# Triangular diagonal blocks of a gated delta rule: 32x32 blocks solved on GpSimd instead of 16x16 blocks with a doubling step on TensorE

## The chip, the cores and the metric

The kernel runs on one core of a Trainium2 chip. The metric is device microseconds of one execution. The kernel before takes 3029.99 us (median of 3 runs, 3028.96 to 3030.83).

## What is computed

One residual layer over 1024 time steps of width 2048: RMSNorm, one combined projection, two branches (an S5 state-space scan and a gated DeltaNet), merge gates, output projection, residual, final RMSNorm. All is float32. The change lies in the DeltaNet branch alone, 8 heads of width 128:

```
a_mat = where(strict, beta * kk * decay, 0)             # per chunk of time steps, strictly lower
sol   = triangular_solve(a_mat, [v*beta, k*beta*exp(gc)], lower, unit_diagonal)
u_c, w_c = sol[..., :dv], sol[..., dv:]
step: v_new = u_i - w_i @ state ; o = qd_i @ state + qk_i @ v_new
      state = state * gl_i + kd_i^T @ v_new
```

The kernel does not solve for the right-hand sides. It builds the inverse of the unit triangular matrix (I + A) for each chunk and multiplies with it. Its chunks have 128 steps.

## The kernel before

**Passes and columns.** The sequence is worked off in two passes of 512 steps. A pass runs through a list of column blocks of 128 projection columns (k, q, v, z and two gate columns for each head, and one u or zs column); each is a row of matmuls on TensorE of 128x512, three for each of 16 slices of the contraction (weights split in a high and a low part: high x high, high x low, low x high). The weights come by SP DMAs of 512 KB into three buffers `raw` (line 397), ScalarE copies the high part `whi` and VectorE subtracts for the low part `wlo`, five buffers each, prepared four chunks (of four slices) ahead (`LA`, line 391).

**What runs between the columns.** All other work stands in lanes (line 444), as Python generators. After each slice of a column, `pump` (line 475) lets every lane issue its next piece, if a planner's clock (class `Clock`, lines 31 to 91, with the costs of lines 140 to 143) says that what the piece before made is ready by TensorE's planned time, 0.2 us of margin added (`step`, line 455). So the order on each engine is fixed when the program is built, by planned times; on the chip, semaphores hold back what comes too early. A DMA is planned at 0.45 us of issue on SP and some 1.1 us of latency after its transfer; a GpSimd two-input operation at 0.14 us and 2.1 ns for each element of its row. Before the columns of head i, `drain` (lines 1529, 1530) issues what is left of the heads up to i-2.

**Lane prep, `d_prep` (line 1090), once for each head and pass, 16 times in all.** Each works on 4 chunks of 128 steps at once, so on 128x512 tiles:
1. GpSimd and TensorE make the decay factors E. Once the head's q column is there, TensorE transposes k (`pK`), ScalarE squares q and k, and TensorE sums the squares by a product with `ones` (`pQ`, line 1116).
2. TensorE multiplies k with k and q (`pA`), VectorE masks and scales: LU, for each chunk c the matrix LU[s, c, t], upper triangular, as the transpose of A.
3. LU goes to DRAM (`lu_d`, line 1139), and the 32 diagonal blocks of 16x16 (8 in each of 4 chunks) come back with one block in each of 32 partitions.
4. GpSimd inverts the blocks by 15 steps of substitution, two operations each (line 1152), and copies a transposed form.
5. Both forms go to DRAM (`tu_d`, two DMAs), and both come back into 128x512 tiles `Tm` and `U` (two DMAs, lines 1173 and 1174). Off the blocks these DRAM areas hold zeros, written once at the start (`zero_tu`).
6. TensorE doubles the blocks from 16 to 32: 16 products of 32x32 (`pG`), two VectorE operations, 32 products of 32x32 (`pU`, line 1188), eight ScalarE copies of 32x128.
7. TensorE doubles from 32 to 64 (8 and 16 products of 32x32) and from 64 to 128 (4 and 4 of 64x64).

**Lane chain, `d_chain` (line 1240),** takes U, which is now the full inverse, through the recurrence over the four chunks. Lane s5 carries the scans of the other branch, mainly on VectorE.

The profile's times for these pieces all have line 135, the recording helper, so they are told apart by tile names: `M` is the block in which all of the head's tiles (LU, E, mi, U, v, kq) lie, `p` a PSUM bank.

Of the kernel before, what the change touches and what calls it, by code (L numbers as in the profile page):

```python
# [93 lines left out]
class Timed:  # L94
# [3 lines left out]
    def __getattr__(self, name):  # L98
# [45 lines left out]
        "memset": _VF, "reciprocal": {"V": (0.07, 8.3e-3)}, "iota": _VG, "matmul": None, "transpose": None, "dma_start": None}  # L144
# [3 lines left out]
def kernel(  # L148
# [90 lines left out]
    off16 = cpool.tile([P, 2, 16], F32, name="off16")  # L239
    id32 = cpool.tile([P, 32], F32, name="id32")  # L240
    G.memset(off16, 0.0)
    for b in range(4):
        s32 = slice(32 * b, 32 * b + 32)
        G.tensor_copy(id32[s32, :], ident[s32, s32])
        G.memset(off16[s32, 0, :], -1.0)
        G.affine_select(off16[s32, 0, :], off16[s32, 0, :], pattern=[[0, 16]], compare_op=ALU.is_ge,
                        fill=0.0, base=-16, channel_multiplier=1)
# [29 lines left out]
    lu_d = [dram.tile([4, 129, P], F32, name=f"lu_d{i}") for i in range(2)]  # L277
    tu_d = [[dram.tile([4, 129, P], F32, name=f"tu_d{i}{j}") for j in range(2)] for i in range(2)]
# [717 lines left out]
    def d_views(mb):  # L996
# [93 lines left out]
    def d_prep(h, ps_):  # L1090
# [48 lines left out]
        SP.dma_start(rows(lud), LU)  # L1139
        yield  # L1140
        mif = mi.rearrange("p c n -> p (c n)")
        Ef = E.rearrange("p c n -> p (c n)")
        ba = mif[0:32, 0:256].rearrange("p (i m) -> p i m", i=16)
        btm = mif[0:32, 256:512].rearrange("p (i m) -> p i m", i=16)
        bx = Ef[0:32, 0:256].rearrange("p (i m) -> p i m", i=16)
        bu = Ef[0:32, 256:512].rearrange("p (i m) -> p i m", i=16)
# [33 lines left out]
        B4 = [slice(32 * b, 32 * b + 32) for b in range(4)]  # L1180
# [502 lines left out]
```

## Time and profile before

| | |
|---|---|
| median of 3 runs | 3029.99 us |
| the profiled execution | 3029.73 us |
| its span | 3027.8 us |
| TensorE busy | 2974.2 us (98%) |
| VectorE, ScalarE, GpSimd busy | 55%, 38%, 15% |
| mean granted clock | 0.993 |

One execution was profiled. Its span runs from the first to the last instruction; 1.9 us of the execution's time lie around it. Busy time of TensorE is the time in which at least one matmul is under way, and since matmuls overlap, a row's own mean is longer than the time that it takes from the engine. What a group of small matmuls takes is therefore read from the starts of the rows on both sides of it.

### The profile page before, as it was taken

How to read it: one execution, taken by the hardware profiler on the slowest of the kernel's cores; microseconds unless marked ns; L12 is line 12 of the kernel's file. 1: busy time of each engine (PE TensorE's matmuls, PEld its weight loads, DVE VectorE, ACT ScalarE, POOL GpSimd, SP SyncE). 2: the span in 40 equal slices, each digit the busy share in tenths (PEclk: the TensorE clock that was granted, in tenths of full speed). 3: DMA queues.
4: the chain of work that ended last, by engine and by line, in shares of the span. 5: the costliest groups of instructions: out<-in, count | busy, mean ns of one | idle time of the engine just before them, and what ended most of it. 6: DMA issues, size and time to landing. Idle time of an engine off the chain costs nothing.

```text
span 3027.8 us, 42544 instructions
## 1 busy us (share of the span) xinstructions
PE 2974.2 (98%) x16030; PEld 2391.6 (79%) x16030; DVE 1662.4 (55%) x3082; ACT 1152.2 (38%) x2483; POOL 449.3 (15%) x857
## 2 busy tenths in 40 slices
PE   8989999999999999999999999999999999999998
PEld 6877777777777888888878777777777788888887
DVE  5746676777777522553454575567557633226542
ACT  5434544554454222334333333333433322223331
POOL 4412222122200000000033221222112000000000
PEclk9999999999999999999999999999999999999999
DMA  6525444444445644446354344444444464445541
GB/s 168 133 57 154 122 121 130 111 117 122 133 135 166 191 122 120 144 134 238 119 160 134 108 114 115 133 114 117 119 126 120 123 207 122 122 122 153 197 151 56
DMA packets 582143, 405.02 MB, mean 134 GB/s; under 512 B 55161, under 2 KB 515122, under 8 KB 580018
## 3 DMA queue, kind: packets, MB, share of 16 engines
q1 hardware_dynamic: 579634, 393.92, 45.3%
q0 software_dynamic: 2304, 8.39, 0.8%
q8 instruction: 126, 2.06, 0.3%
q14 instruction: 79, 0.65, 0.1%
HBM read 335.66 MB, written 66.58 MB: 133 GB/s over the span
## 4 chain that ended last, share of the span: by engine, by line
PE 85%; DVE 7%; POOL 2%; ACT 2%; issue 1%; DMA 1%; SPq 0%; DVEq 0%; POOLq 0%; ACTq 0%
PE p L135 85%; DVE G0a L135 2%; POOL M L135 2%; DVE M L135 2%; DVE wlo L135 1%; DVE tmp L135 1%; ACT M L135 1%; DMA raw<-in_w_in_dram 0%; DVE Y L135 0%; POOL smalls L135 0%; DMA M<-tu_d 0%; SPq L135 0%; ACT whi L135 0%; ACT L135 0%; ACT tmp L135 0%
## 5 line engine op out<-in xcount | busy, mean ns | idle before, releaser
L135 PE MATMUL p<-X,whi 128*128 128x512 f32 (+1 forms) x4432 | 1398.7, 398 | 1.9 <-DVE whi L135 0.8
L135 DVE TENSOR_TENSOR wlo<-raw,whi 128x512 fp32r<-128x512 f32 x920 | 631.0, 698 | 700.9 <-ACT whi L135 700.1
L135 PEld LDWEIGHTS p<-X,whi 128*128 128x128 f32 (+1 forms) x4432 | 802.8, 188 | 177.1 <-issue 19.9
L135 PE MATMUL p<-X,wlo 128*128 128x512 f32 (+1 forms) x2184 | 854.2, 391 | 8.0 <-DVE wlo L135 7.9
L135 ACT ACTIVATE whi<-raw 128x512 fp32r<-128x512 f32 x917 | 557.7, 625 | 512.6 <-PE p L135 485.0
L135 PE MATMUL p<-Y,whi 128*128 128x512 f32 (+1 forms) x1808 | 568.8, 396 | 1.9 <-ACT whi L135 1.1
L135 PEld LDWEIGHTS p<-X,wlo 128*128 128x128 f32 x2184 | 411.7, 189 | 97.6 <-DVE wlo L135 9.1
L135 PEld LDWEIGHTS p<-Y,whi 128*128 128x128 f32 (+1 forms) x1808 | 329.9, 187 | 72.8 <-ACT whi L135 2.6
L135 PE MATMUL p<-Y,wlo 128*128 128x512 f32 x896 | 349.8, 390 | 0.0
L135 POOL TENSOR_SCALAR smalls<-smalls 128x4 f32<-128x4 f32 (+1 forms) x58 | 15.7, 270 | 1603.8 <-DVE smalls L135 1109.4
L135 ACT ACTIVATE tmp<-p 128x512 f32<-128x512 f32 x160 | 95.5, 597 | 401.8 <-PE p L135 391.9
L135 POOL TENSOR_TENSOR M<-M 32x28 f32<-32x28 f32 (+8 forms) x492 | 190.7, 388 | 289.4 <-DMA M<-lu_d 194.2
L135 DVE TENSOR_TENSOR G0a<-G0a 128x256 f32<-128x256 f32 (+1 forms) x432 | 212.3, 528 | 3.4
L135 PEld LDWEIGHTS p<-M 32*32 32x32 f32 (+2 forms) x3072 | 153.5, 123 | 72.6 <-ACT M L135 32.7
L135 PEld LDWEIGHTS p<-Y,wlo 128*128 128x128 f32 x896 | 168.3, 188 | 36.5 <-DVE wlo L135 0.4
L135 PE MATMUL p<-M 32*32 32x32 f32 (+3 forms) x3072 | 187.2, 215 | 7.5 <-ACT M L135 3.8
L135 ACT ACTIVATE M<-p 32x128 f32<-32x128 f32 (+3 forms) x337 | 99.3, 298 | 159.9 <-PE p L135 156.2
L135 DVE SCALAR_TENSOR_TENSOR tmp<-tmp,vec 128x512 f32<-128x512 f32 x144 | 115.6, 803 | 11.9 <-ACT tmp L135 8.5
L135 DVE TENSOR_TENSOR_SCAN G0a<-rho,scar,G0a 128x256 f32<-128x256 f32 x128 | 89.7, 742 | 0.0
L135 DVE TENSOR_TENSOR G0a<-p,G0a 128x512 f32<-128x512 f32 x128 | 82.0, 682 | 13.4 <-PE p L135 10.8
L135 PE MATMUL p<-whi,G0a 128*128 128x512 f32 x280 | 88.5, 391 | 0.0
L135 PE MATMUL p<-whi,X 128*128 128x512 f32 x256 | 82.2, 393 | 0.0
(210 smaller groups left out, 2655.4 us busy)
## 6 DMA issues: line engine op xcount, KB each, us to landing
raw<-in_w_in_dram SPq DMA_DIRECT2D x324, 512.0 KB, 4.0
raw<-in_w_out_dram SPq DMA_DIRECT2D x56, 512.0 KB, 3.9
raw<-in_dn_w_up_dram SPq DMA_DIRECT2D x32, 512.0 KB, 4.1
raw<-in_s_w_up_dram SPq DMA_DIRECT2D x32, 512.0 KB, 3.8
td_d<-tmp SPq DMA_DIRECT2D x32, 256.0 KB, 2.0
M<-tu_d SPq DMA_DIRECT2D x32, 256.0 KB, 3.8
cs_d<-G0a SPq DMA_DIRECT2D x32, 256.0 KB, 2.3
yg_d<-G0a SPq DMA_DIRECT2D x64, 128.0 KB, 2.4
```

The lines of the kernel that those rows point to most:

```text
L135: return f(*a, **k)
```

## The change

The diagonal blocks that GpSimd inverts are 32x32 instead of 16x16, and step 6, the doubling from 16 to 32, is gone.

- LU's 16 diagonal blocks (4 in each chunk) are written by four DMAs, one for each group of 32 partitions, so that each block lies as 4 KB in one piece. Each block is read into eight partitions: 128 partitions with 4 KB each, over E and mi, which now lie side by side.
- Each partition solves four of a block's 32 columns: 31 steps of two operations on 128 partitions, with 4 x 31 elements in a row at first and 4 x 1 in the end. The right-hand side is the identity, which one more DMA reads from DRAM into the first quarter of U; the second quarter holds the products.
- One form of the result is written and read back (one DMA each instead of two). VectorE makes the other by a transpose of 32x32 blocks, 128x512 in one instruction.
- The constants `off16` and `id32` are no longer made, two of four areas are zeroed at the start, and the planner gets a cost for VectorE's transpose.

```diff
-        SP.dma_start(rows(lud), LU)
-        yield
...
-        SP.dma_start(ba, diag_blocks(lud))
-        G.memset(mif[0:32, 256:512], 0.0)
-        G.memset(mif[0:32, 256:512:17], 1.0)
-        yield
-
-        for j in range(15):
-            n = 15 - j
-            a = ba[:, j, j + 1:16].unsqueeze(2).broadcast_to([32, n, j + 1])
-            b = btm[:, j:j + 1, 0:j + 1].broadcast_to([32, n, j + 1])
-            tt(bx[:, 0:n, 0:j + 1], a, b, MUL, eng=G)
-            tt(btm[:, j + 1:16, 0:j + 1], btm[:, j + 1:16, 0:j + 1], bx[:, 0:n, 0:j + 1], SUB, eng=G)
+        for b in range(4):
+            SP.dma_start(part(lud, b * 1024, (32, 32), (4096, 4), (1, 32)),
+                         LU[32 * b:32 * b + 32, :, 32 * b:32 * b + 32])
+        yield
+
+
+        lb = dw["Emi"].rearrange("p (j t) -> p j t", j=32)
+        Uf = U.rearrange("p c n -> p (c n)")
+        iu, ix = (Uf[:, i * P:(i + 1) * P].rearrange("p (m t) -> p m t", m=4) for i in range(2))
+        SP.dma_start(dw["Emi"], part(lud, 0, (1024, 16), (0, 8), (1, 1024)))
+        SP.dma_start(Uf[:, 0:P], part(idg_d, 0, (0, 16), (P, 8), (1, P)))
+        yield
+        for j in range(31):
+            n = 31 - j
+            a = lb[:, j:j + 1, j + 1:32].broadcast_to([P, 4, n])
+            b = iu[:, :, j:j + 1].broadcast_to([P, 4, n])
+            tt(ix[:, :, 0:n], a, b, MUL, eng=G)
+            tt(iu[:, :, j + 1:32], iu[:, :, j + 1:32], ix[:, :, 0:n], SUB, eng=G)
             if j % 3 == 2:
                 yield
-        G.tensor_copy(bu, btm.rearrange("p i m -> p m i"))
-        yield
-        SP.dma_start(diag_blocks(tud[0]), btm)
-        SP.dma_start(diag_blocks(tud[1]), bu)
+        SP.dma_start(part(tud, 0, (4128, 16), (512, 8), (P, 4), (1, 32)), iu)
...
-        SP.dma_start(Tm, rows(tud[0]))
-        SP.dma_start(U, rows(tud[1]))
-        yield
-
-        pG = bank(5)
+        SP.dma_start(U, rows(tud))
+        yield
+        V.transpose(Tm.rearrange("p c n -> p (c n)"), U.rearrange("p c n -> p (c n)"))
         gs = mi
-        g3 = mi[:, :, 0:32]
...
-        for b in B4:
-            for c in range(4):
-                PE.matmul(pG[b, c * 32:(c + 1) * 32], lhsT=LU[b, c, b], rhs=Tm[b, c, b], start=True, stop=True)
...
-        for b in B4:
-            S.activation(U[b, :, b], pU[b, 0:P].rearrange("p (c n) -> p c n", c=4), AF.Copy)
-        for b in B4:
-            S.activation(Tm[b, :, b], pU[b, P:2 * P].rearrange("p (c n) -> p c n", c=4), AF.Copy)
         yield
```

TensorE's queue at the end of the prep of head 4 in the second pass, before: `M_1700_13069` is the head's block, `p_2185_16984` the bank of the column under way.

```order
L135 MATMUL p_2185_16984<-X_1462_11596,wlo_16955 128x512
L135 MATMUL p_2194_17060<-M_1700_13069 32x32 x16
L135 MATMUL p_2185_16984<-X_1462_11596,whi_16985 128x512 x2
L135 MATMUL p_2185_16984<-X_1462_11596,wlo_16986 128x512
L135 MATMUL p_2185_16984<-X_1462_11596,whi_16985 128x512 x2
L135 MATMUL p_2185_16984<-X_1462_11596,wlo_16986 128x512
L135 MATMUL p_2198_17095<-M_1700_13069 32x32 x32
L135 MATMUL p_2185_16984<-X_1462_11596,whi_16985 128x512 x2
```

The same place now, where the first of the small products are those of the doubling from 32 to 64:

```order
L135 MATMUL p_2172_16745<-X_1446_11355,wlo_16747 128x512
L135 MATMUL p_2184_16832<-M_1684_12828 32x32 x8
L135 MATMUL p_2185_16843<-Y_1445_11354,whi_16771 128x512 x2
L135 MATMUL p_2185_16843<-Y_1445_11354,wlo_16772 128x512
L135 MATMUL p_2185_16843<-Y_1445_11354,whi_16771 128x512 x2
L135 MATMUL p_2185_16843<-Y_1445_11354,wlo_16772 128x512
L135 MATMUL p_2188_16855<-M_1684_12828 32x32 x16
L135 MATMUL p_2185_16843<-Y_1445_11354,whi_16771 128x512 x2
```

The groups of 16 and 32 products are gone. The group of 8 stands 183 column matmuls of 128x512 after the write of LU; before, the group of 16 stood 106 after it.

SP's queue from the write of LU on, before (`raw` are weights, `cs_d`, `zd_d` and `td_d` belong to other lanes):

```order
L135 DMA lu_d_124<-M_1700_13069 128x4x128
L135 DMA raw_16842<-in_w_in_dram 128x8x128
L135 DMA M_1700_13069<-lu_d_124 32x16x16
L135 DMA G0a_12916<-cs_d 128x512
L135 DMA raw_16895<-in_w_in_dram 128x8x128
L135 DMA zd_d<-tmp 128x512
L135 DMA raw_16952<-in_w_in_dram 128x8x128
L135 DMA G0a_12916<-cs_d 128x512
L135 DMA td_d<-tmp 128x512
L135 DMA tu_d_126<-M_1700_13069 32x16x16
L135 DMA tu_d_127<-M_1700_13069 32x16x16
L135 DMA raw_17015<-in_w_in_dram 128x8x128
```

The 16x16 blocks are read back two rows after LU is written, and six DMAs stand between that read and the writes to `tu_d`.

SP's queue now, from the write of LU on (`idg_d` holds the identity):

```order
L135 DMA lu_d_109<-M_1684_12828 32x4x32 x4
L135 DMA raw_16448<-in_w_in_dram 128x8x128
L135 DMA M_1684_12828<-lu_d_109 128x1x1024
L135 DMA M_1684_12828<-idg_d 128x1x128
L135 DMA raw_16494<-in_w_in_dram 128x8x128
L135 DMA G0a_12675<-cs_d 128x512
```

The write is four DMAs, and the read is followed by one of the identity. Further on in the same queue, at the end of the GpSimd work:

```order
L135 DMA yg_d<-G0a_12675 64x2x256 x4
L135 DMA raw_16720<-in_w_in_dram 128x8x128
L135 DMA td_d<-tmp 128x512
L135 DMA raw_16769<-in_w_in_dram 128x8x128
L135 DMA tu_d_111<-M_1684_12828 16x32x32
L135 DMA M_1684_12828<-tu_d_111 128x4x128
L135 DMA raw_16813<-in_w_in_dram 128x8x128
```

Between the read from `lu_d` and the write to `tu_d` now stand sixteen DMAs, the identity's read among them, and `tu_d` is written and read by one DMA each instead of two.

VectorE's queue at the same place, now:

```order
L135 TENSOR_TENSOR wlo_16797<-raw_16661,whi_16796 128x512
L135 TENSOR_TENSOR wlo_16816<-raw_16720,whi_16815 128x512
L135 STREAM_TRANSPOSE M_1684_12828<-M_1684_12828 128x512
L135 TENSOR_TENSOR wlo_16845<-raw_16720,whi_16844 128x512
L135 TENSOR_TENSOR wlo_16895<-raw_16769,whi_16894 128x512
L135 TENSOR_TENSOR wlo_16921<-raw_16769,whi_16920 128x512
```

The transpose stands between low parts of weights, and waits there for the read from `tu_d`. Before, two short operations on the products of 16x16 blocks stood in such a place.

## Rows read from the trace of the kernel before

**Rows 1.** The page: span, TensorE's busy time, chain by engine.

```profile
span 3027.8 us, 42544 instructions
PE 2974.2 (98%) x16030; PEld 2391.6 (79%) x16030; DVE 1662.4 (55%) x3082; ACT 1152.2 (38%) x2483; POOL 449.3 (15%) x857
PE 85%; DVE 7%; POOL 2%; ACT 2%; issue 1%; DMA 1%; SPq 0%; DVEq 0%; POOLq 0%; ACTq 0%
```

**Rows 2.** Timeline, TensorE, last head: start, length, engine, operation.

```profile
2334.61 0.39 PE L135 MATMUL p<-X,wlo 128*128 128x512 f32 x1
2334.93 0.89 PE L135 MATMUL p<-M 32*32 32x32 f32 x32
2335.75 0.73 PE L135 MATMUL p<-X,whi 128*128 128x512 f32 x2
2336.33 0.39 PE L135 MATMUL p<-X,wlo 128*128 128x512 f32 x1
2336.56 0.62 PE L135 MATMUL p<-X,whi 128*128 128x512 f32 x2
2337.02 0.39 PE L135 MATMUL p<-X,wlo 128*128 128x512 f32 x1
2337.34 1.91 PE L135 MATMUL p<-M 32*32 32x32 f32 x64
2339.17 0.74 PE L135 MATMUL p<-X,whi 128*128 128x512 f32 x2
2339.75 0.39 PE L135 MATMUL p<-X,wlo 128*128 128x512 f32 x1
```

**Rows 3.** Groups by shape, TensorE: count, busy us, mean ns, idle before.

```profile
L135 PE MATMUL p<-M 32*32 32x32 f32 x2304 | 64.6, 193 | 2.4 <-DMA M<-tu_d 1.9 <-ACT M L135 0.2
```

**Rows 4.** Timeline, SP, head 4 of the second pass.

```profile
2001.31 0.37 SPq L135 DMA_DIRECT2D lu_d<-M  x1
2003.61 0.56 SPq L135 DMA_DIRECT2D M<-lu_d  x1
2021.63 1.01 SPq L135 DMA_DIRECT2D tu_d<-M  x2
2024.12 0.93 SPq L135 DMA_DIRECT2D M<-tu_d  x2
2050.94 1.76 SPq L135 DMA_DIRECT2D us_d<-G0a  x4
```

**Rows 5.** Timeline, GpSimd, the solve in three heads (30 operations each).

```profile
704.85 14.72 POOL L135 TENSOR_TENSOR M<-M 32x15 f32<-32x15 f32 x30 [16.86 <-DMA M<-lu_d]
1626.94 12.01 POOL L135 TENSOR_TENSOR M<-M 32x15 f32<-32x15 f32 x30 [14.04 <-DMA M<-lu_d]
2007.42 14.18 POOL L135 TENSOR_TENSOR M<-M 32x15 f32<-32x15 f32 x30 [17.72 <-DVE G0a L135]
```

**Rows 6.** Timeline, TensorE, head 4 of the second pass.

```profile
2028.22 0.87 PE L135 MATMUL p<-M 32*32 32x32 f32 x32 [0.23 <-DMA M<-tu_d]
```

**Rows 7.** Groups by shape, GpSimd: the solve's shapes, and a wider one.

```profile
L135 POOL TENSOR_TENSOR M<-M 32x60 f32<-32x60 f32 x64 | 29.0, 454 | 5.0
...
L135 POOL TENSOR_TENSOR dhl<-gth,causal 128x256 fp32r<-128x256 f32 x32 | 24.8, 776 | 15.5 <-PE p L135 15.5
...
L135 POOL TENSOR_TENSOR M<-M 32x15 f32<-32x15 f32 x64 | 19.3, 301 | 255.9 <-DMA M<-lu_d 194.2 <-DVE G0a L135 35.7 <-DVE scar L135 17.0
```

**Rows 8.** The page, groups: GpSimd's solve, 480 of 492 operations.

```profile
L135 POOL TENSOR_TENSOR M<-M 32x28 f32<-32x28 f32 (+8 forms) x492 | 190.7, 388 | 289.4 <-DMA M<-lu_d 194.2
```

**Rows 9.** DMA issues: KB each, median us to landing.

```profile
raw<-in_w_in_dram SPq DMA_DIRECT2D x324, 512.0 KB, 4.0
...
M<-tu_d SPq DMA_DIRECT2D x32, 256.0 KB, 3.8
...
us_d<-G0a SPq DMA_DIRECT2D x64, 64.0 KB, 1.7
```

**Rows 10.** Groups by shape, VectorE, whole span.

```profile
L135 DVE TENSOR_TENSOR wlo<-raw,whi 128x512 fp32r<-128x512 f32 x920 | 631.0, 698 | 700.9 <-ACT whi L135 700.1
...
L135 DVE TENSOR_TENSOR M<-M,tmp 128x512 f32<-128x512 f32 x44 | 30.1, 691 | 1.1
...
L135 DVE TENSOR_SCALAR G0a<-G0a 128x256 f32<-128x256 f32 x64 | 19.3, 301 | 2.2
```

**Rows 11.** Groups by shape, VectorE, 2360 to 3028 us (hardly any GpSimd work).

```profile
L135 DVE TENSOR_TENSOR wlo<-raw,whi 128x512 fp32r<-128x512 f32 x220 | 146.5, 689 | 206.2 <-ACT whi L135 206.2
```

**Rows 12.** Waits of TensorE: us, times, longest.

```profile
PE p L135 <- POOL tmp L135: 5.3, 1, 5.3
PE p L135 <- DMA M<-tu_d: 1.9, 3, 1.5
```

**Rows 13.** Groups by shape, TensorE: the sums of squares.

```profile
L135 PE MATMUL p<-ones,M 128*128 128x1 f32 x128 | 16.2, 248 | 9.7 <-ACT M L135 9.7
```

**Rows 14.** Timeline, TensorE, one of these waits.

```profile
2088.55 1.05 PE L135 MATMUL p<-ones,M 128*128 128x1 f32 x8 [1.73 <-ACT M L135]
```

**Rows 15.** Stretches: length, busy us (count) of PE, PEld, DVE, ACT, POOL, clock, DMA.

```profile
1882.20:1888.90 6.70, 6.70 (x22) 4.33 (x22) 2.36 (x7) 1.16 (x6) 2.92 (x7) 0.50 0.22 67
...
2090.40:2093.70 3.30, 3.30 (x12) 1.84 (x12) 1.52 (x6) 0.00 (x0) 2.22 (x6) 0.50 0.05 15
...
1700.00:2360.00 660.00, 647.49 (x3965) 506.60 (x3963) 395.37 (x734) 247.03 (x613) 145.12 (x305) 0.98 0.44 119
```

More of the change, by code (lines that the diff above doesn't have):

```diff
@@ L143 @@
         "tensor_reduce": _VG, "activation": _VG, "tensor_tensor_scan": {"V": (0.07, 1.28e-3)},
-        "memset": _VF, "reciprocal": {"V": (0.07, 8.3e-3)}, "iota": _VG, "matmul": None, "transpose": None, "dma_start": None}
+        "memset": _VF, "reciprocal": {"V": (0.07, 8.3e-3)}, "iota": _VG, "matmul": None, "transpose": {"V": (0.07, 1.04e-3)}, "dma_start": None}
 @with_exitstack
@@ L238 @@
                     channel_multiplier=1)
[L239 to L247, printed above, removed]
     after_r = cpool.tile([P, P], F32R, name="after_r")
@@ L275 @@
     cs_d = dram.tile([32, P, 512], F32, name="cs_d")
-    lu_d = [dram.tile([4, 129, P], F32, name=f"lu_d{i}") for i in range(2)]
-    tu_d = [[dram.tile([4, 129, P], F32, name=f"tu_d{i}{j}") for j in range(2)] for i in range(2)]
+    lu_d = [dram.tile([4, 4, 1024], F32, name=f"lu_d{i}") for i in range(2)]
+    tu_d = [dram.tile([4, 129, P], F32, name=f"tu_d{i}") for i in range(2)]
+    idg_d = dram.tile([1, 32, 32], F32, name="idg_d")
     st_d = dram.tile([8, P, P], F32, name="st_d")
@@ L1008, in d_views @@
             dw["set"].append(s)
-        dw["E"] = tk(512).rearrange("p (c n) -> p c n", c=4)
         dw["LU"] = tk(512).rearrange("p (c n) -> p c n", c=4)
-        dw["mi"] = tk(512).rearrange("p (c n) -> p c n", c=4)
+        dw["Emi"] = tk(1024)
+        dw["E"] = dw["Emi"][:, 0:512].rearrange("p (c n) -> p c n", c=4)
+        dw["mi"] = dw["Emi"][:, 512:1024].rearrange("p (c n) -> p c n", c=4)
         dw["ch"] = tk(512)
@@ L1172, in d_prep @@
         yield stored
-        SP.dma_start(Tm, rows(tud[0]))
-        SP.dma_start(U, rows(tud[1]))
+        SP.dma_start(U, rows(tud))
         yield
-        pG = bank(5)
+        V.transpose(Tm.rearrange("p c n -> p (c n)"), U.rearrange("p c n -> p (c n)"))
         gs = mi
-        g3 = mi[:, :, 0:32]
-        B4 = [slice(32 * b, 32 * b + 32) for b in range(4)]
-        for b in B4:
-            for c in range(4):
-                PE.matmul(pG[b, c * 32:(c + 1) * 32], lhsT=LU[b, c, b], rhs=Tm[b, c, b], start=True, stop=True)
-        tt(g3, pG[:, 0:P].rearrange("p (c n) -> p c n", c=4),
-           off16.rearrange("p a c -> p (a c)")[:, None, :].broadcast_to([P, 4, 32]), MUL)
-        tt(g3, g3, id32[:, None, :].broadcast_to([P, 4, 32]), ADD)
-        yield
-        pU = bank(2)
-        for b in B4:
-            for c in range(4):
-                PE.matmul(pU[b, c * 32:(c + 1) * 32], lhsT=g3[b, c, :], rhs=U[b, c, b], start=True, stop=True)
-                PE.matmul(pU[b, P + c * 32:P + (c + 1) * 32], lhsT=U[b, c, b], rhs=g3[b, c, :],
-                          start=True, stop=True)
-        for b in B4:
-            S.activation(U[b, :, b], pU[b, 0:P].rearrange("p (c n) -> p c n", c=4), AF.Copy)
-        for b in B4:
-            S.activation(Tm[b, :, b], pU[b, P:2 * P].rearrange("p (c n) -> p c n", c=4), AF.Copy)
         yield
@@ L1314, in zero_tu @@
     def zero_tu():
-        for a in tu_d:
-            for b in a:
-                SP.dma_start(rows(b), ztile.rearrange("p (c n) -> p c n", c=4))
+        for b in tu_d:
+            SP.dma_start(rows(b), ztile.rearrange("p (c n) -> p c n", c=4))
+        SP.dma_start(idg_d[0], ident[0:32, 0:32])
     def out_gen(yr, oss, r0):
```

9 lines of the change are left out of this document (removed).

## The prediction

> **What bounds the kernel now.** I read the page first: TensorE is busy for 2974.2 of 3027.8 us, and 85% of the chain that ended last is its own [rows 1]. So work taken from TensorE shortens the span nearly one for one, and work added elsewhere costs nothing as long as TensorE does not come to wait for it. Next the timeline around a small product, for what it takes from the engine; then SP's, GpSimd's and TensorE's rows of one head in their order, for the path from the write of LU to the first product that needs `Tm`; last the waits of TensorE. In head 4 of the second pass that path is tight: the read from `tu_d` issued at 2024.12 ends TensorE's wait at 2028.22, 0.23 us late [rows 4, 6]. Over all 16 heads TensorE waited for `tu_d` 1.9 us [rows 12]. So there is hardly any room there, and everything hangs on how the new, longer path compares with the new place of its consumer.
>
> The profiled execution took 3029.73 us, 1.9 us more than its span, and 0.3 us less than the median. I sum against 3029.7.
>
> **What TensorE loses.** In the last head, where it waited for nothing, the columns' rows go by a fixed step: from the start of a `wlo` row to that of the next `whi` row 0.23 us, from a `whi` row of two to the next `wlo` row 0.46 (2336.33, 2336.56, 2337.02). Around the first group the two steps are 1.14 and 0.58, so it takes 1.14 - 0.23 + 0.58 - 0.46 = 1.03 us; around the second 2.15 and 0.58, so 2.15 - 0.23 + 0.12 = 2.04 [rows 2]. The two groups are 32 + 64 = 96 of the 144 records of a head (2304 / 16) [rows 3]. Together 3.07 us a head, 49.1 us in 16 heads. The bound from below is their busy time alone: 96/144 of 64.6 is 43 us. The waits for `tu_d`, 1.9 us, are those of the removed products and go with them, if nothing takes their place: -51.0.
>
> **What GpSimd gains.** 62 operations instead of 30, with 4n elements in a row, n from 31 to 1, each twice: 8 x 496 = 3968 elements instead of 1360. A line through the rows of 15 elements (301 ns) and of 256 (776) gives 271 ns and 1.97 ns an element; before each of these operations the engine sat 0.078 us (5.0 us in 64) [rows 7]. Before: 30 x 0.271 + 1360 x 0.00197 + 29 x 0.078 = 13.1 us. The trace has 12.0 to 14.7 [rows 5], and on average, from 480/492 of 190.7 over 16, 11.6 + 2.3 = 13.9 [rows 8]. Now: 62 x 0.271 + 3968 x 0.00197 + 61 x 0.078 = 16.8 + 7.8 + 4.8 = 29.4 us; times 13.9/13.1, 31 us. From below 29.4 x 12.0/13.1 = 27, from above 33 by the slowest head, and 33 too if every operation takes what one of 60 elements does, 454 + 78 ns. That it is 128 partitions and no longer 32 I put at nothing, since the row of 256 elements has 128.
>
> The Trainium skill speaks against such work here: the page "GPSIMD Engine Reference", section "Performance versus the Vector engine", puts a two-input operation at about 2.6 cycles an element, 2.17 ns by its clock as an estimate. By that the solve takes 32 instead of 31 us, ten heads are short instead of five, and the sum below comes to about 2994; rows 7 show 1.97 ns.
>
> **The new path, and its budget.** From the first write of LU: four writes of a quarter each; `us_d` is written by four such DMAs in 1.76 us, 0.44 each, landing 1.7 us after issue [rows 4, 9]. The read is so issued after 3 x 0.44 + 1.7 = 3.0 us (2.3 before: 2001.31 to 2003.61). It brings 512 KB like a weight load, 4.0 us [rows 9], and the identity's read, one issue of 0.44 behind, may land last: GpSimd starts at 7.5 (before at 2007.42, 6.1). It ends at 38.5. The write to `tu_d` and its landing took 2.5 us with two writes (2021.63 to 2024.12), half a us between their issues: 2.0. The read took 4.0 with two; with one I take 3.6 (median 3.8). The transpose is in no row: 0.69 like one-pass work of 128x512 [rows 10], not under 0.3 (half the size in the fastest mode seen) and not over 1.4, plus 0.15 for semaphores. Need: 45.0 us. Bounds, with 27 to 33 for the solve and 1 us either way for the DMAs: 40 to 48.5.
>
> The budget is what TensorE has queued between that write and the first 32x32 product. In head 4 of the second pass it was 106 column matmuls, at 0.227 (0.68 to 0.69 for three, rows 2), and 1.9 us of transposes and scan matmuls: 26.0, where the trace has 26.9 with the wait of 0.23 [rows 4, 6]. The count plus 0.5 is so what the chip has. Counted in the same way in the changed program, that head has 183 column matmuls, 43.9, and the 16 heads in order of size have, with the 0.5: 42.3, 42.6, 44.2, 44.4, 44.4, 45.3, 45.6, 45.7, 45.8, 45.9, 46.1, 48.0, 48.2, 49.1, 49.5, 52.4. Against a need of 45.0 five heads are short, by 2.7, 2.4, 0.8, 0.6 and 0.6: 7.1 us of new waits.
>
> A wait costs more than itself. After the 1.73 us wait at 2088.55 the granted clock was 0.50 (1.2 GHz, not 2.4) for 3.3 us at least, in another head for 6.7 [rows 14, 15]; half of that is lost, some 1.7 to 1.9 us after a wait. For the two longer waits I add 4 us. New waits: +11, at a need of 40 nothing, at 48.5 some 60.
>
> **What else moves.** SP has two issues more in a head (eight for six). Its write to `tu_d` now waits for a longer solve, with weight loads queued behind; these run three buffers ahead and the split parts four chunks (48 column matmuls, 10.9 us), so a hold of 5 us is hidden; beyond some 10 it would not be. VectorE's transpose waits in its queue for the read, with low parts of weights behind it, under the same cover; it loses two operations and gains one. ScalarE loses eight copies a head. Both sit idle for far more than that. At the start GpSimd makes fewer constants; TensorE's first wait is for it (5.3 us, rows 12), but the columns wait for x and the weights: nothing, at best -3.
>
> The sums of squares: TensorE waits 9.7 us there [rows 13], six waits of 1.2 to 1.7 us in the second pass, and after each the clock falls: five times 3.3 us and once 6.7 at the least, 12 us lost. They come where the scans' VectorE work stands ahead of q's last operation. Counting VectorE's queued work against TensorE's between q's column and the product, those six heads have 1.4 to 2.2 us of room, the others over 3.4. In the changed program two heads have 0.9, two of the first pass 1.5 and 2.3, the rest 2.8 or more. So two to four such waits instead of six, at 3.6 us each: -7 to -14. I take -8; the bounds are -22 and +14.
>
> **Sum.** 3029.7 - 51.0 + 11 - 8 = 2981.7, so 2982.
>
> **The rivals.**
> 1. Slower: the solve is late in nearly every head, and TensorE waits at the doubling from 32 to 64. For it: the planner counts 2.1 ns an element and 0.14 us a piece, 17 us for what I put at 31, and budgets are close to the need. Against it: the planner's pieces are spread (every sixth operation waits for planned time), so the place of the write to `tu_d` is already 25 to 34 us behind. At a need of 47.5 eleven heads are short, 30 us and 19 for the clock: 49, as much as is saved. There it decides. At 49 (solve 35) it is 48 + 19 = 67, without the gain at the sums of squares: 3046.
> 2. VectorE becomes late: GpSimd's busy time rises by some 17 us a head, and the operations of both lengthen each other, so that waits like those at the sums of squares come in all 16 heads, ten more at 3.6: 3029.7 - 51.0 + 11 + 36 = 3026. For it: VectorE is busy 395 of 660 us in the second pass's heads [rows 15]. Against it: a low part takes 698 ns on average over the span and 689 where GpSimd hardly works [rows 10, 11]. The Trainium skill, "SBUF — State Buffer", section "Who interferes with whom", has the one that comes second wait for the other's whole instruction when VectorE reads two SBUF inputs; by that rule the added GpSimd time can at worst all fall on VectorE, and the spread of 12.0 to 14.7 us of one solve agrees with a lock of that kind on GpSimd's side.
> 3. All is hidden: the need is 41 or less and the waits at the sums of squares go: 3029.7 - 51.0 - 22 = 2957.
> That the change does not remove what it says is excluded by the order: the groups of 16 and 32 products are not there.
>
> **How the numbers follow.** Forecast 0.60, with its own range 2962 to 3012 (need 43 to 46.5, the sums of squares from -16 to +4); rival 1 0.17; rival 2 0.13; rival 3 0.10. The range for 8 in 10 takes in rival 3's edge, rival 2 and the decision point of rival 1: 2957 to 3034. A measurement here can tell about 0.2%, 6 us. Faster than 3024: the forecast, rival 3 and a few hundredths of rival 2, 0.73. Within 6 us: most of rival 2, 0.09. Slower: 0.18.
>
> **What would show it.** In the trace of the changed kernel: no rows of 32 and 64 records of 32x32; GpSimd's 62 operations in 28 to 33 us; from the first write of LU to the first product 42 to 50 us; TensorE's waits there (for VectorE's transpose) in about five heads, 7 us in sum, the longest under 4; the sums of squares waited for in two to four heads. I am wrong if the solve takes over 34 us, if the DMAs around it take over 16, or if TensorE waits for weights behind SP's or VectorE's held queue.

## The result, and the profile after

The changed kernel takes 3011.98 us, the median of four runs (3008.99 to 3021.00), against 3029.47 for the kernel before beside it (four runs, 3027.76 to 3030.83): a ratio of 0.9948, 95% interval 0.9930 to 0.9965. It is faster, by 17.5 us where I forecast 48. Its four runs spread over 12 us, the slowest at a mean granted clock of 0.984 and the fastest at 0.988; those of the kernel before spread over 3 us. The profiled execution took 3009.36 us.

The page after, span and busy times, against [rows 1]:

```profile
span 3007.7 us, 39850 instructions
PE 2935.3 (98%) x14494; PEld 2363.6 (79%) x14494; DVE 1678.5 (56%) x3066; ACT 1121.1 (37%) x2361; POOL 670.0 (22%) x1308
```

TensorE has 16030 - 14494 = 1536 = 16 x 96 records less, as foreseen, and is busy for 38.9 us less. But the span is only 20.1 us shorter, so TensorE idles more. The groups of the 32x32 products and of the sums of squares (count, busy us, mean ns, idle before), against [rows 3, 13]:

```profile
L135 PE MATMUL p<-M 32*32 32x32 f32 x768 | 21.3, 206 | 26.4 <-DVE M L135 26.4
L135 PE MATMUL p<-ones,M 128*128 128x1 f32 x128 | 15.5, 242 | 1.7 <-ACT M L135 1.7
```

The 32x32 products that stay, those of the step from 32 to 64, now wait 26.4 us for VectorE's transpose, in 11 of 16 heads: 2.00, 2.76, 3.17, 0.35, 2.89, 2.44, 4.69, 1.94, 2.35, 1.73 and 2.10 us. The sums of squares wait 1.7 us instead of 9.7.

The path of the head with the longest wait, in the second pass (start, length; SP's issues, GpSimd's solve, VectorE's transpose, TensorE's first product), against [rows 4 to 6]:

```profile
1777.53 1.74 SPq L135 DMA_DIRECT2D lu_d<-M  x4
1780.43 0.55 SPq L135 DMA_DIRECT2D M<-lu_d  x1
1781.02 0.59 SPq L135 DMA_DIRECT2D M<-idg_d  x1
1819.20 0.56 SPq L135 DMA_DIRECT2D tu_d<-M  x1
1821.36 0.37 SPq L135 DMA_DIRECT2D M<-tu_d  x1
```

```profile
1786.21 32.96 POOL L135 TENSOR_TENSOR M<-M 128x124 f32<-128x124 f32 x62 [2.07 <-DMA M<-idg_d]
```

```profile
1825.32 0.71 DVE L135 STREAM_TRANSPOSE M<-M 128x512 f32<-128x512 f32 x1 [6.79 <-DMA M<-tu_d]
```

```profile
1826.09 0.87 PE L135 MATMUL p<-M 32*32 32x32 f32 x16 [4.69 <-DVE M L135]
```

From the first write to the product 48.6 us pass. Over the 16 heads the time from the first write of LU to the transpose's end, called the needed time from here on, is 48.2 us on the mean (44.9 to 52.7). GpSimd starts 5.8 us behind the read's issue, and what ends its wait is the identity's read, the last of the two. The issues' rows (KB, median us to landing) beside [rows 9], and GpSimd's solve beside [rows 8]:

```profile
raw<-in_w_in_dram SPq DMA_DIRECT2D x324, 512.0 KB, 4.0
...
M<-lu_d SPq DMA_DIRECT2D x16, 512.0 KB, 5.5
```

```profile
L135 POOL TENSOR_TENSOR M<-M 128x32 f32<-128x32 f32 (+30 forms) x1004 | 434.5, 433 | 267.1 <-DMA M<-idg_d 142.3
```

The replicating read is as large as a weight load and takes 5.5 us instead of 4.0; why, no run here shows.

Stretches of half clock after four of the waits (length, busy us and count of PE, PEld, DVE, ACT, POOL, granted clock, DMA), against [rows 15]:

```profile
828.95:842.60 13.65, 13.65 (x76) 9.33 (x76) 3.34 (x6) 3.12 (x9) 0.00 (x0) 0.50 0.22 58
525.17:528.58 3.41, 3.41 (x22) 2.36 (x21) 1.29 (x2) 1.77 (x4) 0.00 (x0) 0.50 0.35 105
1825.65:1842.71 17.06, 16.62 (x93) 12.27 (x94) 1.77 (x3) 4.11 (x11) 0.00 (x0) 0.50 0.36 109
1941.70:1945.11 3.41, 3.41 (x39) 2.31 (x38) 0.00 (x0) 0.48 (x2) 0.00 (x0) 0.50 1.10 348
```

Eight of the eleven waits are followed by such a stretch: 3.4 us five times, 6.8, 13.65 and 17.06, together 54.6 us. Half of that is lost: in the third stretch a column matmul takes 0.43 us from its start to the next one's, where [rows 2] have 0.23.

```profile
1839.38 0.63 PE L135 MATMUL p<-Y,wlo 128*128 128x512 f32 x1
1839.81 1.05 PE L135 MATMUL p<-Y,whi 128*128 128x512 f32 x2
```

**Where the 20 us came from.** Over the whole span the clock was at 0.50 for 71.3 us, before for 45.4. With half of a stretch counted as lost:

| part | forecast | measured, span | how |
|---|---|---|---|
| the removed groups | -49.1 | -51.8 | busy -38.9, less the +12.9 that the clock added to it |
| waits for `tu_d` | -1.9 | -2.0 | gone |
| waits at the first 32x32 product, their clock | +11 | +53.7 | 26.4 + 54.6/2 |
| sums of squares, their clock | -8 | -19.9 | -8.0 and six stretches, 23.9/2 |
| a 7.7 us wait for a `wlo` at 227 us, its clock | 0 | -9.5 | 7.7 to 1.6, and 6.8/2 |
| rest | 0 | +9.4 | 6.4 in waits of under 2.5 us each, 1.8 + 1.0 at the ends, rounding |

### The profile page after: what moved, and what is told of

It reads as the page before. It is cut to its first block, busy times and chain, and to the rows that moved or that the text cites. A ratio compares the mean times of both kernels' runs of the same rounds, so it can differ in the third digit from the quotient of the medians.

```text
span 3007.7 us, 39850 instructions
## 1 busy us (share of the span) xinstructions
PE 2935.3 (98%) x14494; PEld 2363.6 (79%) x14494; DVE 1678.5 (56%) x3066; ACT 1121.1 (37%) x2361; POOL 670.0 (22%) x1308
## 4 chain that ended last, share of the span: by engine, by line
PE 71%; POOL 12%; DVE 6%; DMA 4%; issue 4%; ACT 2%; SPq 1%; DVEq 0%; POOLq 0%; ACTq 0%
PE p L135 71%; POOL M L135 11%; DVE G0a L135 2%; DVE M L135 2%; DMA M<-idg_d 1%; DMA M<-tu_d 1%; DVE wlo L135 1%; DVE tmp L135 1%; ACT M L135 1%; DMA tu_d<-M 1%; SPq L135 1%; DVE Y L135 0%; ACT whi L135 0%; ACT L135 0%; DMA raw<-in_w_in_dram 0%
## 5 line engine op out<-in xcount | busy, mean ns | idle before, releaser
L135 DVE TENSOR_TENSOR wlo<-raw,whi 128x512 fp32r<-128x512 f32 x920 | 639.5, 709 | 720.7 <-ACT whi L135 719.7
L135 POOL TENSOR_TENSOR M<-M 128x32 f32<-128x32 f32 (+30 forms) x1004 | 434.5, 433 | 267.1 <-DMA M<-idg_d 142.3
L135 DVE TENSOR_TENSOR G0a<-G0a 128x256 f32<-128x256 f32 (+1 forms) x432 | 222.2, 550 | 6.6 <-ACT G0a L135 3.1
L135 PEld LDWEIGHTS p<-M 32*32 32x32 f32 (+2 forms) x1536 | 115.7, 147 | 94.6 <-DVE M L135 42.7
L135 PE MATMUL p<-M 32*32 32x32 f32 (+3 forms) x1536 | 146.1, 246 | 34.8 <-DVE M L135 30.1
L135 ACT ACTIVATE M<-p 32x128 f32<-32x128 f32 (+4 forms) x209 | 64.5, 314 | 182.8 <-PE p L135 174.4
L135 POOL TENSOR_TENSOR dhl<-gtl,causal 128x256 fp32r<-128x256 f32 x32 | 22.9, 715 | 339.6 <-PE p L135 339.0
```

The costliest lines, as they stand in the source:

```text
L135: return f(*a, **k)
```

## The experiments

Each kernel is timed against the kernel before beside it (3029 to 3033 us). "Half clock" is the sum of all such stretches in the trace. The first four were to tell whether the waits at the first product cost what is missing, and what takes them away.

| kernel | median us | ratio, 95% interval | waits at first product | half clock |
|---|---|---|---|---|
| kernel before | 3029 to 3033 | 1 | 2.0 (for `tu_d`) | 45.4 |
| changed kernel | 3011.98 | 0.9948 (0.9930 to 0.9965) | 26.4 | 71.3 |
| read and transpose later | 3003.94 | 0.9904 (0.9882 to 0.9925) | 29.2 | 90.1 |
| a quarter of the solve | 2955.95 | 0.9757 (0.9740 to 0.9774) | 0 | 21.5 |
| before, no doubling | 2966.69 | 0.9784 (0.9770 to 0.9799) | 1.6 | 28.8 |
| planner's costs | 3234.93 | 1.0669 (1.0651 to 1.0686) | see below | 378.0 |
| transpose alone, 5 us | 2944.36 | 0.9720 (0.9705 to 0.9734) | 0 | 20.2 |
| early identity, half reads | 3007.51 | 0.9917 (0.9897 to 0.9937) | 22.2 | 111.5 |
| both | 2969.94 | 0.9805 (0.9788 to 0.9823) | 0 | 26.3 |
| transpose alone, 2.5 us | 2971.11 | 0.9812 (0.9790 to 0.9834) | 11.0 | 37.8 |
| transpose alone, 7.5 us | 2953.37 | 0.9746 (0.9731 to 0.9760) | 0 | 24.7 |
| before, reads' user later | 2999.97 | 0.9901 (0.9886 to 0.9916) | 0 | 24.5 |
| half reads, same order | 2986.79 | 0.9864 (0.9841 to 0.9886) | 14.5 | 48.2 |

**A quarter of the solve** (each GpSimd operation on one of the four columns, charged in the planner as before, so that the order is the changed kernel's).

```
-            tt(ix[:, :, 0:n], a, b, MUL, eng=G)
-            tt(iu[:, :, j + 1:32], iu[:, :, j + 1:32], ix[:, :, 0:n], SUB, eng=G)
+            planned("G", ...)   # charged as the full size
+            nc.gpsimd.tensor_tensor(ix[:, 0:1, 0:n], lb[:, j:j + 1, j + 1:32], ..., op=MUL)
+            planned("G", ...)
+            nc.gpsimd.tensor_tensor(iu[:, 0:1, j + 1:32], iu[:, 0:1, j + 1:32], ix[:, 0:1, 0:n], op=SUB)
```

> The changed kernel in the same order on TensorE, VectorE, ScalarE and SP, but each of the 62 GpSimd operations works on one of its four columns (the planner is still charged for four; three quarters of the inverse are left as the identity). Theory A: the solve takes 22 to 25 us instead of 31.5, the path 39 to 41, no waits at the 32x32 products, and nothing else moves: 2955 to 2970, which is what 49 us of removed TensorE work and the waits gone at the sums of squares give. Theory B (the waits come from the reads and writes around the solve, or from VectorE held up by GpSimd): waits of over 10 us in sum remain there, 2985 or more.

The solve took 25.3 us on the mean instead of 31.5, a little over what I expected. The needed time fell to 44.9 us only, not to 39 to 41: the read from `tu_d` now goes out 4.3 us behind the write on the mean, in the changed kernel 2.5. It was enough all the same, by 0.6 us in the tightest head; with the same order nothing waits at the first product:

```profile
L135 PE MATMUL p<-M 32*32 32x32 f32 x768 | 19.0, 194 | 0.0
```

It is 54.0 us faster than the changed kernel, profiled execution against profiled execution (2955.33, 3009.36). TensorE's waits fell by 30.6 us and half clock by 49.8, of which half is 24.9: together 55.5. So the waits and the clock behind them cost what the table above puts on them.

**Read and transpose later.** The obvious cure: all that follows the write to `tu_d` 5 us later on the planner's clock.

```
-        yield stored
+        yield stored + 5.0
         SP.dma_start(U, rows(tud))
```

> The changed kernel, with the read from tu_d planned 5 us later, so that the transpose and the first 32x32 product stand later in their queues (47.5 to 53.1 us of queued TensorE work after the first write of LU, 41.8 to 51.9 before). Theory A (the consumer comes too early for a path of some 48 us; each wait costs itself and a stretch at half clock): the 26.4 us of waits at the 32x32 products fall under 5, the stretches at half clock from 27 us lost to under 15, and the time to 2965 to 2980; the sums of squares may cost up to 15 again, since their room shrinks to 1.8 to 2.4 us in five heads. Theory B (the lateness is only moved: U comes 5 us later for the recurrence and the scans): waits of the same size at other products, 3000 or more.

The waits did not go (ten heads):

```profile
L135 PE MATMUL p<-M 32*32 32x32 f32 x768 | 21.3, 206 | 29.2 <-DVE M L135 29.2
```

SP's queue in one of the heads (start, length) shows the reason at its clearest:

```profile
1837.09 0.58 SPq L135 DMA_DIRECT2D tu_d<-M  x1
1837.72 3.15 SPq L135 DMA_DIRECT2D us_d<-G0a  x4
1840.96 2.55 SPq L135 DMA_DIRECT2D yg_d<-G0a  x4
1843.56 1.33 SPq L135 DMA_DIRECT2D raw<-in_w_in_dram  x2
1844.93 1.16 SPq L135 DMA_DIRECT2D M<-tu_d  x1
```

The read was moved with its user: it stands behind other issues now and goes out 7.8 us behind the write, where 2.2 had been enough. On the mean of the heads it goes out 4.3 us behind the write instead of 2.5, and the transpose begins 5.6 us behind the read instead of 3.8; the solve and its start add 1.0. So the needed time grew from 48.2 to 52.8 us, and the time from the first write to the product, without the wait, by no more than that, from 47.0 to 51.5. My first theory failed on that.

**The transpose alone later.** So the read keeps its place, and only what uses it moves.

```
         SP.dma_start(U, rows(tud))
-        yield
+        yield clock.last + 5.0
         V.transpose(...)
```

> The read from tu_d keeps its place; the VectorE transpose and all that follows it is placed 5 us later on the planner's clock. Counted in the order, the TensorE work between the first lu_d write and the first 32x32 product is then 48.5 to 58 us (median 50.3), against 41.8 to 51.9 (median 45.2) in the changed kernel. Theory A (the needed time is the 48 us that the changed kernel showed, and does not depend on where the product stands): waits at the first 32x32 product fall from 26.4 us to under 6, half-clock stretches from 71 us to 45 or less, and the time to 2955 to 2972 us. Theory B (the needed time grows with the place, as it grew from 48.6 to 53.3 us where the read was placed later too): waits stay over 20 us and the time at 2995 us or more.

2944.36 us: 85 us under the kernel before, 38 under my forecast for the change, below my first theory's 2955 to 2972 too, and the fastest of all. Page, the products and TensorE's longest waits (us, times, longest):

```profile
span 2940.9 us, 39846 instructions
PE 2906.7 (99%) x14494; PEld 2350.5 (80%) x14494; DVE 1680.4 (57%) x3066; ACT 1113.7 (38%) x2353; POOL 673.5 (23%) x1308
```

```profile
L135 PE MATMUL p<-M 32*32 32x32 f32 x768 | 19.0, 194 | 0.0
```

```profile
PE p L135 <- DVE M L135: 8.7, 5, 5.2
PE p L135 <- POOL tmp L135: 3.1, 1, 3.1
```

TensorE's waits are 25.3 us in all (changed kernel 63.5), and what is left of them stands mostly at the program's start. The product now stands 0 to 6 us behind the transpose's end, without a wait.

**2.5 and 7.5 us** in the place of 5.0: `yield clock.last + 2.5` and `yield clock.last + 7.5`.

> As the kernel with the transpose placed 5 us later, but 2.5 us. The TensorE work counted between the first lu_d write and the first product is 45.5 to 51.7 us (median 47.8) against a need of 48.6 us on the mean. Theory A (the time is lost to this wait and to the clock behind it): about half of the heads are short by up to 3 us, waits at the first product 8 to 14 us, half-clock stretches between 20 and 71 us, time between the two neighbours, 2960 to 2985 us. Theory B (the gain of the 5 us version came from another order of the work, not from the wait): no relation to the hold, 2944 to 2955 us, or 3000 us or more.

> As the kernel with the transpose placed 5 us later, but 7.5 us; the count is 50.3 to 62.9 us (median 52.5), so every head has 1.7 us or more to spare. Theory A: no waits at the first product, and nothing more to win: 2940 to 2955 us. Theory B (the later product makes the recurrence of the head late): waits of the chain's first products or of the 64x256 and 128x256 products of 5 us or more in sum that the 5 us version does not have, and 2960 us or more.

At 2.5 us four heads still wait, 4.58, 5.35, 0.44 and 0.67 us, two of them longer than the 3 us that I had counted with, and the time is between its neighbours:

```profile
L135 PE MATMUL p<-M 32*32 32x32 f32 x768 | 20.1, 199 | 11.0 <-DVE M L135 11.0
```

At 7.5 nothing waits there, and the time is 9 us over that at 5.0, within my first theory's 2940 to 2955. Waits for ScalarE's `G0b` and `M` come up (4.1 and 4.0 us in sum against 1.8 and 1.0), of the kind and size that my second theory named. But others shrink: in all TensorE waits 4.1 us more, and half clock is 4.5 us longer. That makes some 6 of the 9 us.

```profile
PE p L135 <- ACT G0b L135: 4.1, 7, 1.4
PE p L135 <- ACT M L135: 4.0, 5, 1.9
```

**The kernel before, its user later.** A control: how much of the 85 us is the other place and not the change? Nothing else is changed.

```
         SP.dma_start(U, rows(tud[1]))
-        yield
+        yield clock.last + 5.0
```

> The kernel before, with all that follows its two reads from tu_d placed 5 us later on the planner's clock; nothing of the change is in it. Theory A (the later place is worth what the waits there cost: 2.0 us in four heads, no half clock behind them): 3022 to 3030 us. Theory B (the later place brings a luckier order by itself, so that much of the 85 us that the changed kernel with this edit gained over the kernel before is not the change's): 3010 us or less.

30 us, which I had not expected: my first theory fell. The waits for `tu_d` were 2.0 us; what went is elsewhere. TensorE's waits fell by 17.4 us in all and half clock by 20.9, half of which is 10.4: the 28 us between the two profiled executions. The sums of squares wait 1.7 us instead of 9.7, and the 7.7 us wait for a `wlo` is not there. First TensorE's busy time and the group, then the stretch in which TensorE of the kernel before stood (columns as above):

```profile
PE 2963.8 (99%) x16030; PEld 2389.6 (80%) x16030; DVE 1653.3 (55%) x3082; ACT 1156.8 (39%) x2489; POOL 449.7 (15%) x857
L135 PE MATMUL p<-ones,M 128*128 128x1 f32 x128 | 15.5, 242 | 1.7 <-ACT M L135 1.7
```

```profile
220.00:235.00 15.00, 15.00 (x70) 12.30 (x69) 14.30 (x19) 5.06 (x10) 11.55 (x15) 1.00 0.51 149
```

TensorE is busy for all of the 15 us, at full clock. VectorE's queue shows what had held the low part: in the kernel before twelve operations on `Y` stand in one row ahead of it (first line, 14.71 us); with the shift they go by threes, with low parts between them (second line).

```profile
211.00 14.71 DVE L135 TENSOR_TENSOR Y<-Y 128x1024 f32<-128x1024 f32 x12
211.08 3.61 DVE L135 TENSOR_TENSOR Y<-Y 128x1024 f32<-128x1024 f32 x3
```

So a shift of the later pieces against VectorE's queue takes these waits away. The change did it by its own shift, and got 29 us for it (table above); with the waits gone on both sides the change is worth 55 us (0.9720 against 0.9901): busy time falls from 2963.8 to 2906.7 us, 57.1, of which 2.2 are the clock's.

**Before, without the doubling.** The kernel before with its step from 16 to 32 on TensorE (two groups of products, two VectorE operations, eight copies) taken out, 22 lines; the output lacks that step.

```
-        g3 = mi[:, :, 0:32]
...
-                PE.matmul(pG[b, c * 32:(c + 1) * 32], lhsT=LU[b, c, b], rhs=Tm[b, c, b], start=True, stop=True)
...
-            S.activation(Tm[b, :, b], pU[b, P:2 * P].rearrange("p (c n) -> p c n", c=4), AF.Copy)
-        yield
```

> The kernel before, with the doubling from 16 to 32 left out (48 products of 32x32, two VectorE operations, eight ScalarE copies a head; the inverse lacks these blocks), all else as before. It prices the removed TensorE work alone. Theory A: 49 us of TensorE, so 2973 to 2985 against 3029.5 (the waits for tu_d stay). Theory B (the small products were partly hidden, or the time comes back as waits since the path behind it gets no longer): 3000 or more.

It saved 65.9 us, more than I expected.

```profile
PE 2915.6 (98%) x14494; PEld 2347.6 (79%) x14494; DVE 1651.4 (56%) x3050; ACT 1115.1 (38%) x2355; POOL 459.0 (15%) x857
```

Busy time fell by 58.6 us, of which 8.3 are half of the 16.6 us less at half clock: 50.3 for the groups, my 49.1 within 1.2 us. The rest is the sums of squares again (5.5 us of waits instead of 9.7) and their clock.

**Early identity, half reads; and both edits.** The identity is read ahead of the writes to `lu_d`, and 512 KB become two reads of 256, so that GpSimd can begin on rows 0 to 15.

```
+        SP.dma_start(Uf[:, 0:P], part(idg_d, ...))     # ahead of the four writes
...
-        SP.dma_start(dw["Emi"], part(lud, 0, (1024, 16), (0, 8), (1, 1024)))
-        SP.dma_start(Uf[:, 0:P], part(idg_d, ...))
+        for i in (0, 512):
+            SP.dma_start(dw["Emi"][:, i:i + 512], part(lud, i, (1024, 16), (0, 8), (1, 512)))
```

> The identity for the solve is read ahead of the four lu_d writes, and the 512 KB read from lu_d is issued as two of 256 KB (rows 0 to 15, then 16 to 31). The planner also moves: the TensorE work counted between the first write and the first product falls by 1.8 us in the median (45.2 to 43.8 with the start of the count moved behind the identity's read). Theory A (the size of the read and the identity behind it made the 6.1 us to the solve's start): GpSimd starts 3.8 to 4.8 us after the first read's issue, the needed time falls from 48.6 to about 46.8, and the time stays within 2998 to 3015 us, since the count fell as well. Theory B (the start waits for the four writes to land and the read's fixed latency, not for its size): GpSimd starts 5.5 us or more after the issue, waits at the first product grow to 40 us or more, and the time to 3020 us or more.

> Both edits: identity ahead of the writes, the read in two halves, and the transpose with what follows it 5 us later on the planner's clock; the count is 45.7 to 53.2 us (median 48.1). Theory A: needed time about 46.8 us, waits at the first product under 3 us, time 2950 to 2968 us, at or a few us below the kernel with the later transpose alone. Theory B (needed time grows with the place): waits over 15 us, 2990 us or more.

The solve starts 8.0 us behind the first write instead of 9.6, and the needed time falls from 48.2 to 46.2. But the planner, charged with smaller reads, sets the product earlier as well (1.4 us in the median of the counts), and the waits hardly shrink; half clock is 40 us longer, and the time is hardly better than the changed kernel's (3007.51 against 3011.98). With both edits no head waits, and yet it is 26 us slower than with the later transpose alone: half clock is 6.1 us longer, waits 12.4 us longer (for ScalarE's `M` 9.2 us against 1.0, for `v_d` 3.3). That is 15 of the 21 us between the profiled executions, and the time, 2969.94, lies just outside my 2950 to 2968. The order is another one; what in it costs this I did not take apart.

**Half reads, same order.** The same reads, identity first, but charged in the planner as the changed kernel's, so that TensorE's order is the same row for row.

```
-        SP.dma_start(dw["Emi"], part(lud, 0, (1024, 16), (0, 8), (1, 1024)))
-        SP.dma_start(Uf[:, 0:P], part(idg_d, 0, (0, 16), (P, 8), (1, P)))
+        clock.run("Q", ...)     # both charged as before
+        nc.sync.dma_start(Uf[:, 0:P], eye)
+        for i in (0, 512):
+            nc.sync.dma_start(dw["Emi"][:, i:i + 512], part(lud, i, (1024, 16), (0, 8), (1, 512)))
```

> TensorE's order is that of the changed kernel, word for word. Only the reads for the solve differ: the identity is issued first, then the 512 KB of lu_d as two reads of 256 KB (rows 0 to 15, then 16 to 31), so that GpSimd can start on the first half. Theory A (the start of the solve, 6.1 us behind the first read's issue, was set by the size of the read and by the identity behind it): the start comes 1.2 to 2 us sooner, the needed time falls to about 47, the eleven waits at the first product shrink by that each, to some 8 to 14 us in sum, and half-clock stretches fall below 60 us; 2970 to 2992 us. Theory B (the start waits for the four writes to land and for a read's fixed time): the start comes less than 0.6 us sooner, waits stay at 20 us or more, and the time at 3000 us or more.

The same head as above, on SP and GpSimd:

```profile
1763.82 1.74 SPq L135 DMA_DIRECT2D lu_d<-M  x4
```

```profile
1771.07 32.23 POOL L135 TENSOR_TENSOR M<-M 128x124 f32<-128x124 f32 x62 [0.64 <-DMA M<-lu_d]
```

```profile
L135 PE MATMUL p<-M 32*32 32x32 f32 x768 | 19.6, 198 | 14.5 <-DVE M L135 14.5
```

From the first write to the solve's start 7.3 us, where it was 8.7 (1777.53 to 1786.21). On the mean of the heads 8.4 against 9.6, needed time 47.2 against 48.2, waits 14.5 us against 26.4, half clock 48.2 against 71.3; 25 us faster. So 1.0 us of needed time was worth 25 us: with eleven heads short each microsecond is paid eleven times, and about once more by the clock. Whether the size of the read or the identity's place behind it held the solve, this run does not separate.

**The planner's costs.** GpSimd's cost of an operation in the planner raised to what the trace shows, from (0.14, 2.1e-3) to (0.36, 2.4e-3) us for the fixed part and an element.

```
-_VG = {"V": (0.07, 1.04e-3), "G": (0.14, 2.1e-3), "S": (0.05, 0.9e-3)}
+_VG = {"V": (0.07, 1.04e-3), "G": (0.36, 2.4e-3), "S": (0.05, 0.9e-3)}
```

> The changed kernel with the planner's cost of a GpSimd two-input operation raised from 0.14 us and 2.1 ns an element to 0.36 and 2.4, which gives 31.8 us for the 62 operations, as measured (31.5). The write to tu_d, the read, the transpose and the first product all stand later (54.6 us and more of queued TensorE work, against a path of 48). Theory A: no waits at the 32x32 products, little half clock, 2955 to 2970, below e1_later by some 10 since SP and VectorE are not held and the sums of squares have room in all heads but two. Theory B (prep is now so long that the recurrence or the next head comes late): waits elsewhere, 2990 or more.

223 us slower than the changed kernel, on the side of the second theory. TensorE's waits rose to 231 us; the longest:

```profile
PE p L135 <- DVE G0a L135: 84.8, 20, 7.2
PE p L135 <- DVE M L135: 51.1, 36, 5.2
PE p L135 <- issue: 34.3, 8, 8.7
```

The waits are 168 us longer than in the changed kernel, and TensorE is busy for 57 us longer, with 378 us of half clock. The table of costs holds for all of GpSimd's work, so every lane moved; the longest waits in sum are for VectorE's `G0a`, a tile of other lanes. Which lane held which, no run shows. Right durations in the planner are not by themselves a better order.

## Why the prediction was wrong, step by step

- **What TensorE loses** (-49.1): right. 50.3 by the kernel without the doubling, 51.8 by the changed kernel's own busy time, 54.9 with the waits gone on both sides.
- **The solve** (31 us, 27 to 33): 31.5 on the mean, 28.8 to 33.0. Right, but for the make-up: with 64 elements in a row on the mean an operation takes 433 ns, with 16 (the quarter) 331, so 2.1 ns an element and 297 fixed; I had 1.97 and 271. A line through the 31 sizes of the changed kernel's solve alone gives about 2.3 and 284, with the later transpose about 1.9 and 313, through the quarter's small sizes about 3.6 and 275, so the rate is known to a few tenths of a ns at best. The Trainium skill, "GPSIMD Engine Reference", section "Performance versus the Vector engine", has 2.6 cycles an element, 2.17 ns by its clock as an estimate; these rows fit it, and do not tell it from my 1.97. The 31 came out only because of the factor 13.9/13.1.
- **The DMAs around the solve**: the first failed step. I had the solve start 7.5 us behind the first write, with "512 KB like a weight load, 4.0 us", and it starts 9.6 behind on the mean: the read goes out after 3.6 instead of 3.0, the replicating read lands after 5.5, the identity's last. Behind the solve, from the write to the transpose, I had 5.6, and it is 6.3. Together 15.9 us where I had 13.1, just under the 16 that I had named as a sign of being wrong. The 0.15 us for semaphores stands in no row; the product follows the transpose's end by 0.06. Needed time 48.2 us on the mean instead of 45.0, within my bounds of 40 to 48.5, near the upper end. The half reads show that this is what it was: 1.0 us less there, 25 us less in all.
- **The waits** (five heads, 7.1 us): eleven heads, 26.4 us, about the number that I gave for a needed time of 47.5 (eleven heads, 30 us). It measured 48.2, and at 48.2 my list of budgets gives twelve heads and 38 us. The list was a little short as well: its mean is 46.2 us, and on the chip the time from the first write to the product, without the wait, is 47.0. The mechanism of rival 1 took place, under a forecast that priced it at its edge.
- **The price of a wait**: the second failed step. I took 1.7 to 1.9 us of lost clock for a wait and 4 us in all, from stretches of 3.3 and 6.7 us. After the changed kernel's waits there are 54.6 us of half clock, half of it lost: 27.3, or 2.5 for each of the eleven. With the 26.4 it is +53.7 where the sum has +11. That is the term that was wrong. Most of its error is the first step's: at my own price, eleven waits with 19 us for the clock, the 26.4 us would have come to 45. The price adds the other 8.
- **The sums of squares** (-8): mechanism right, the size too small. The waits alone fell by 8.0, with the clock 19.9, close to the bound of -22; and I had not looked at the single 7.7 us wait of the first pass, another 9.5. Beyond the -8 of the sum these two gave 21 us and so hid half of what the new waits cost beyond the +11. That the wait for the `wlo` went was luck: nothing in the prediction foresaw it. Without both gains the profiled execution would have been at 3009.4 + 19.9 + 9.5 = 3039, near rival 1's 3046.
- **Rival 2** (VectorE slowed by GpSimd): a `wlo` operation takes 709 ns on the mean against 698 before, and 697 with the quarter of the solve. That is 920 x 11 ns = 10 us of VectorE's time, which VectorE, 56% busy, hides. The Trainium skill, "SBUF — State Buffer", section "Who interferes with whom", has a VectorE instruction with two SBUF inputs contend with a GpSimd instruction that reads SBUF, over a pair of ports that it calls an exclusive lock. Single rows agree: a low part that began 0.07 us behind a GpSimd operation of 1.29 us took 1.76 us and ended 0.54 us after it. On the mean little is left of it: 648 of the 920 low parts have no GpSimd work beside them and take 687 ns, the 249 with GpSimd busy for over half of their time take 762. First the groups, after and with the quarter, then the two rows:

```profile
L135 DVE TENSOR_TENSOR wlo<-raw,whi 128x512 fp32r<-128x512 f32 x920 | 639.5, 709 | 720.7 <-ACT whi L135 719.7
L135 DVE TENSOR_TENSOR wlo<-raw,whi 128x512 fp32r<-128x512 f32 x920 | 628.9, 697 | 754.8 <-ACT whi L135 753.8
```

```profile
459.50 1.29 POOL L135 TENSOR_TENSOR M<-M,causal 128x512 f32<-128x512 f32 x1 [2.45 <-ACT M L135]
459.57 1.76 DVE L135 TENSOR_TENSOR wlo<-raw,whi 128x512 fp32r<-128x512 f32 x1
```

- **SP's held queue**: right, for all that the rows show. Once the program's start is over, TensorE waits for split weights at one place, 1.6 us at 245 to 250 us, and what stood ahead of them was ScalarE's wait for the write to `ft_d`, not a held write to `tu_d`:

```profile
244.22 0.63 ACT L135 ACTIVATE Y<-M 128x512 fp32r<-128x512 f32 x1 [10.74 <-DMA ft_d<-Y]
```

What stays open: why half clock lasts 3.4 us after one wait and 17 after another. The wait of 2.76 us at 525 is followed by 3.4 us of it, that of 2.89 at 827 by 13.65, both with TensorE busy throughout, and that of 2.35 us at 2035 by none. The longer stretch also holds eight 64x256 products of `G0b` beside columns and small products, which the shorter one does not; but the 17.06 us after the 4.69 us wait hold columns and small products alone. No run here takes that apart.

## What to carry to other kernels

Count the path of a moved step in what it must bring and what it must fetch: here a replicated read was not a weight load of the same size. When a wait appears at the consumer, move the consumer alone and leave its transfer where it is: moved together they keep their distance, and here the wait (3003.94 against 2944.36 us). How far to move it was found by trial: 2971 us at 2.5, 2944 at 5.0, 2953 at 7.5. And before a gain is put down to a change, give the old kernel the same shift of its order; here that alone was worth 30 of 85 us.

## What was not expected of the hardware

- After waits of 1.9 to 4.7 us of TensorE the granted clock stayed at 0.50 for 3.4 to 17.1 us in the changed kernel, and up to 23.9 us after a wait of 1.57 us in the kernel with the early identity, with TensorE busy from the end of the wait on: the length of a wait doesn't tell that of the stretch. The longest of them, but for its edges:

```profile
171.80:195.60 23.80, 23.80 (x177) 18.74 (x178) 1.85 (x4) 5.22 (x14) 0.61 (x1) 0.50 0.12 34
```

- Writing 16 rows of a DRAM tile to 128 partitions, each row to eight: 512 KB in 5.5 us, 256 KB in 4.2, where a weight load of 512 KB takes 4.0 in the same kernel.
- VectorE's transpose of 128x512 float32 in 32x32 blocks took 0.71 us, as long as a one-pass operation on that size (0.69 to 0.71).
- GpSimd's two-input operations on 128 partitions: some 297 ns and 2.1 ns an element, from means of 433 ns at 64 elements and 331 at 16. Of a solve of 62 such operations nearly three quarters (62 x 0.297 and 61 x 0.08 of 31.5 us) are the fixed part and the gaps between them.
